# Routing on raw x, with the modulation moved from the tokens into the experts of a hierarchical expert layer

## The chip, the cores and the metric

The kernel runs on one core of a Trainium2 chip. The metric is the device time of one execution in microseconds (us): the median of three runs of the kernel before is 1857.02 us (1854.01 to 1859.16). Engines are called TensorE (PE, matmuls and transposes), VectorE (DVE), ScalarE (ACT), GpSimd (POOL) and SyncE (SP, which issues most DMAs).

## What is computed

The reference is two blocks in a row, over 512 tokens of 1024 numbers in float32. The first block is two layers of attention and is not touched. The second block has two layers, each a mixer followed by a hierarchical mixture of experts; the change is in the latter, which runs once per layer. Cut to that:

```python
def modulate(x, gain, shift, scale):
    return rms_norm_2(x, gain) * (1 + scale) + shift

def hier_moe(h, rg_w, rg_b, re_w, re_b, w_gate, w_up, w_down):
    ...
    g_prob = jax.nn.softmax(t32 @ rg_w + rg_b, axis=-1)
    g_p, g_idx = lax.top_k(g_prob, 1)
    e_logits = (t32 @ re_w + re_b).reshape(n_tok, N_GROUPS, EXPERTS_PER_GROUP)
    e_sel = jnp.take_along_axis(e_logits, g_idx[:, :, None], axis=1)[:, 0]
    top_p, top_i = lax.top_k(jax.nn.softmax(e_sel, axis=-1), TOP_K)
    ...
    def step(acc, xs):
        wg, wu, wd, cw = xs
        y = (jax.nn.silu(t @ wg) * (t @ wu)) @ wd
        return acc + y * cw[:, None], None

h_lat = h_lat + g2 * hier_moe(modulate(h_lat, norm2_g[i], sh2, sc2), *moe_args)
```

There are 16 experts in 4 groups; a token goes to the best group and to the best two of its four experts. An expert is 1024 to 256 (twice, gate and up) and 256 to 1024. With A = gain * (1 + scale), the modulated token is x * rs * A + shift, where rs is one number per token (the reciprocal of its root mean square) and A and shift have one number per column.

## The kernel before, in words

Tokens lie on 128 partitions in four tiles of 128 tokens, x[:, i, :]. Large products are made as three passes over a high and a low part of each operand: `split_to` (L400) writes the high part with a ScalarE copy and the low part with a subtract on VectorE, or on the engine that is passed as `sub`; `mm3` (L347) issues the three matmuls, the two that need only one low part each behind the one of both high parts. Weights come in chunks of 128x1024 (`weights`, L330), in three buffers each for the high and the low part, so that the split of a chunk waits until TensorE is done with the chunk three before it.

`moe` (L1517) does one layer. Its parts, in the order of the work:

- `moe_tables` (L1507) loads, well ahead, the rows A, shift and g2 as broadcast tiles of 128x1024 (tag "mv", three buffers), and small tables; `rw` holds the router's weights.
- The routing is in a block whose order on TensorE, GpSimd, ScalarE and VectorE is the written one (L1783 to L1843). `k.arrive` pulls out the next piece of the mixer before it, whose last matmuls are added to x at L1037. For each tile i: `square` (L1565) sums squares on ScalarE, `scaled` (L1571) multiplies x by A, `turned` (L1544, L1545) transposes that on TensorE and copies it out on ScalarE, `logits` (L1552) and `folded` (L1558) make 20 router logits on TensorE, `rms` takes the reciprocal root in small VectorE steps (L384 to L397), and `modulate` (L1582 on VectorE, or L1584 on ScalarE with L1585 on GpSimd) finishes the token, which SP stores to a DRAM scratch `tscr` (L1587). `route` (L1591 to L1611) ranks the logits, in VectorE operations of at most 80 elements.
- `before`, `spots`, `hot` and `place` (L1618 to L1648) turn the ranks into the list of tokens of each expert; `fetch` (L1670) gathers 128 rows of `tscr` by that list with an indirect DMA from GpSimd. `place(0, ...)` and `fetch` for expert 0 come first, `place(1, 3, ...)` and the fetch for expert 1 behind it. `split0` splits three of the four weight chunks of expert 0 ahead, with the subtract on GpSimd.
- A branch (L1881) handles an expert with over 128 tokens.
- A second block in written order (L1927 to L1932) does five steps of `weigh` (L1683 to L1722, 20 small operations that make the weights of the experts), `turn` of expert 0's tokens, the rest of `weigh`, and `up(0)`.
- Then the experts. `turn` (L1747) transposes the 128 fetched tokens in two halves of 128x512 into PSUM, and `transposed` (L1735) splits each half from PSUM into xTh (ScalarE) and xTl (VectorE). `up` then runs 24 matmuls over four chunks (L350 to L352 into `pss`), `hidden` (L1762 to L1764) makes silu and product, and `down` (L1852) two transposes, eight matmuls (L1865), the weighting into y (L1867, tag "y", four buffers) and `store` (L1847), an indirect DMA that adds y to the output. Here the engines' orders are a planner's, which interleaves `up(e + 1)` with `down(e)`.

## Time and profile before

| | us |
|---|---|
| median of three runs | 1857.02 (1854.01 to 1859.16) |
| the profiled execution, own time | 1858.75 |
| its span | 1857.0 |
| routing and experts of layer 0, about | 1227 to 1445 |
| routing and experts of layer 1, about | 1628 to 1857 |

The rows further down come from one profiled execution and its times are counted from the span's start. A line of a timeline gives start, duration, engine, line of the code, operation, output<-inputs by the program's names, shapes, how many, and in brackets how long the engine was idle before it and what ended that. Back-to-back operations overlap a little, so durations do not add up exactly to the distance of their starts.

### The profile page before, as it was taken

The numbers are of one execution on the slowest core, as the hardware profiler recorded it, in microseconds if no ns is written. First come the engines' busy times: TensorE is split into PE (matmuls) and PEld (weight loads), VectorE is DVE, ScalarE is ACT, GpSimd is POOL, SyncE is SP. The second block draws the span as 40 slices with busy tenths as digits, with TensorE's granted clock in tenths as the row PEclk, the third lists the DMA queues.
The fourth block names the chain that finished last, engine by engine and source line by source line (L and its number), as shares of the span: only waits on it lengthen the run. The fifth ranks groups of instructions, "written<-read, shape, count | busy, mean of one in ns | idle before, by whom it ended". The sixth has DMA issues, their size and how long they took to land. (4 is left out here: it accounts for less than half of the span.)

```text
span 1857.0 us, 25754 instructions
## 1 busy us (share of the span) xinstructions
PE 1705.9 (92%) x9542; PEld 1334.2 (72%) x9542; DVE 1346.4 (73%) x2532; ACT 770.8 (42%) x1345; POOL 278.2 (15%) x242
## 2 busy tenths in 40 slices
PE   7999999999799999999997889987999799969996
PEld 7877777886697777778866767765666587746663
DVE  4577778876646777576677788879877765589774
ACT  4444333333343443323434445553555322145552
POOL 0000000001200000000003452023221122142221
PEclk9999999999999999999998989997999799979998
DMA  5345565664024445554413213147996463169983
GB/s 176 121 135 149 162 206 162 192 193 135 19 73 125 142 143 151 169 165 148 150 46 110 67 47 126 42 170 265 336 341 194 164 215 95 36 247 304 348 295 75
DMA packets 86948, 298.90 MB, mean 161 GB/s; under 512 B 18854, under 2 KB 20694, under 8 KB 78624
## 3 DMA queue, kind: packets, MB, share of 16 engines
q1 hardware_dynamic: 71584, 271.87, 43.8%
q0 software_dynamic: 10704, 19.79, 4.7%
q10 hardware_dynamic: 4528, 5.51, 1.1%
q8 instruction: 78, 1.28, 0.3%
q14 instruction: 54, 0.44, 0.1%
HBM read 280.23 MB, written 24.96 MB: 164 GB/s over the span
## 5 line engine op out<-in xcount | busy, mean ns | idle before, releaser
L401 ACT ACTIVATE whi<-wraw 128x1024 fp32r<-128x1024 f32 (+2 forms) x166 | 171.7, 1036 | 348.1 <-PE psmm L351 241.6
L350 PE MATMUL psmm<-big,whi 128*128 128x512 f32 x672 | 272.9, 406 | 6.8 <-DVE x L668 5.6
L402 DVE TENSOR_TENSOR wlo<-wraw,whi 128x1024 fp32r<-128x1024 f32 (+3 forms) x165 | 200.9, 1219 | 102.3 <-ACT whi L401 89.6
L352 PE MATMUL psmm<-big,wlo 128*128 128x512 f32 x672 | 266.7, 397 | 0.0
L351 PE MATMUL psmm<-big,whi 128*128 128x512 f32 x672 | 266.6, 397 | 0.0
L980 DVE CUSTOM_DVE_ANT_0 wraw<-wraw,sB 128x1024 f32<-128x1024 f32 x96 | 117.1, 1221 | 83.4 <-DMA wraw<-in_mw_dram 82.9
L350 PE MATMUL psmm<-whi,big 128*128 128x256 f32 (+2 forms) x496 | 165.1, 333 | 1.5 <-ACT big L401 1.0
L351 PE MATMUL psmm<-wlo,big 128*128 128x256 f32 (+2 forms) x496 | 160.7, 324 | 4.9 <-DVE wlo L402 4.9
L352 PE MATMUL psmm<-whi,big 128*128 128x256 f32 (+2 forms) x496 | 159.9, 323 | 2.4 <-DVE big L402 2.3
L350 PEld LDWEIGHTS psmm<-big,whi 128*128 128x128 f32 x672 | 127.3, 189 | 35.8 <-issue 4.7
L352 PEld LDWEIGHTS psmm<-big,wlo 128*128 128x128 f32 x672 | 126.9, 189 | 31.1
L351 PEld LDWEIGHTS psmm<-big,whi 128*128 128x128 f32 x672 | 127.4, 190 | 27.9
L1865 PE MATMUL psmm<-wraw,hs 128*128 128x512 f32 x256 | 122.1, 619 | 5.4 <-ACT hs L1857 3.5
L601 POOL DMA_DIRECT2D qk<-rope x40 | 20.5, 515 | 659.2 <-ACT whi L401 286.9
L351 PEld LDWEIGHTS psmm<-wlo,big 128*128 128x128 f32 x496 | 112.1, 226 | 6.2 <-DVE wlo L402 6.0
L352 PEld LDWEIGHTS psmm<-whi,big 128*128 128x128 f32 x496 | 111.5, 225 | 3.2 <-DVE big L402 3.2
L350 PEld LDWEIGHTS psmm<-whi,big 128*128 128x128 f32 x496 | 111.4, 225 | 2.7 <-ACT big L401 1.7
L350 PE MATMUL pss<-whi,xTh 128*128 128x512 f32 x256 | 104.8, 409 | 2.4 <-ACT xTh L401 2.4
L352 PE MATMUL pss<-whi,xTl 128*128 128x512 f32 x256 | 102.4, 400 | 1.7 <-DVE xTl L402 1.7
L351 PE MATMUL pss<-wlo,xTh 128*128 128x512 f32 x256 | 103.4, 404 | 0.0
L856 PEld LDWEIGHTS pspt<-c_ident,pr 128*128 128x128 f32 x512 | 61.3, 143 | 48.2 <-issue 28.9
L402 DVE TENSOR_TENSOR wlo<-bigm,whi 128x1024 fp32r<-128x1024 f32 x64 | 77.9, 1223 | 17.7 <-ACT whi L401 16.2
(384 smaller groups left out, 3659.7 us busy)
## 6 DMA issues: line engine op xcount, KB each, us to landing
wraw<-in_mw_dram SPq DMA_DIRECT2D x96, 512.0 KB
big<-in_me_dram SPq DMA_DIRECT2D x32, 1024.0 KB
bigm<-in_me_dram SPq DMA_DIRECT2D x32, 1024.0 KB
wraw<-in_me_dram SPq DMA_DIRECT2D x64, 512.0 KB
wraw<-in_wqk_dram SPq DMA_DIRECT2D x48, 512.0 KB
wraw<-in_wv_dram SPq DMA_DIRECT2D x24, 512.0 KB
wraw<-in_ow_dram SPq DMA_DIRECT2D x20, 512.0 KB
wraw<-in_wg_dram SPq DMA_DIRECT2D x16, 512.0 KB
```

What stands on the lines that cost most here:

```text
L350: mm(out, lhs[0], rhs[0], start=first, stop=False)
L351: mm(out, lhs[0], rhs[1], start=False, stop=False)
L352: mm(out, lhs[1], rhs[0], start=False, stop=last)
L401: self.nc.scalar.activation(hi, src, AF.Copy)
L402: (sub or self.nc.vector).tensor_tensor(lo, src, hi.bitcast(F32), ALU.subtract)
L601: nc.gpsimd.dma_start(tiles[b][48:80, :], R[b // 4][32 * (b % 4) : 32 * (b % 4) + 32, :])
L856: nc.tensor.transpose(pt[:, j * P : (j + 1) * P], hd.pr[i][:, j * P : (j + 1) * P], ident)
L980: nc.vector.tensor_tensor_reduce(w, w, sB, 1.0, 0.0, ALU.mult, ALU.add, mf[:, j : j + 1])
L1865: nc.tensor.matmul(acc, hs[:, c * P : (c + 1) * P], w[:, c * 512 : (c + 1) * 512], start=c == 0, stop=c == 1)
```

## The change

The router's weights are multiplied by A once (`r3`), so the routing works on raw x: `scaled` is gone, `turned` transposes x itself, with one copy on VectorE and one on ScalarE. What is stored to `tscr` is x * rs (`send`, a scaled copy on ScalarE). A and shift are loaded as columns (`cols`, 128x2x8, one DMA with 4-byte pieces) and are applied in the experts, to the turned tokens, where a column is a partition: eight ScalarE operations of 128x128 per expert (`modulated_`), with the scale and the bias as pointers, into a new tile of tag "y", from which xTh and xTl are then split. The three subtracts of `split0` move from GpSimd to VectorE, two of them into the second block; `place(1, 3, ...)` and the fetch for expert 1 move there too, and `weigh` runs whole behind `turn` and the last `split0`. The order of the first block is rewritten.

```diff
@@ -1498,16 +1498,18 @@
     nc.vector.tensor_tensor(rb, rb, shift, ALU.add)
 
 
-TABLES = ("mv", "iota", "tri", "info", "rw", "fold")
+TABLES = ("mv", "cols", "iota", "tri", "info", "rw", "fold")
 SMALL = ("lg", "sm", "cmp", "rank", "G", "lgr", "gm", "ge", "gsum", "e2", "w1", "w2", "sec", "We", "Ws",
-         "Ab", "pos", "pos16", "most", "over", "oh", "row", "spread", "lgT", "ix", "ws", "vinf", "vpos", "ivx", "ivw",
+         "Ab", "pos", "pos16", "most", "over", "oh", "row", "spread", "lgT", "ix", "ws", "vinf", "vpos", "ivx", "ivw", "sq2",
          "rs_v2", "rs_y2", "rs_h2", "rs_u2")
 
 
 def moe_tables(k, L, rows):
 
     small = lambda shape, nm, dt=F32: k.t(shape, nm, 1, dt)
-    tables = [brow(k, rows[L], j, ("mv", 3)) for j in (4, 3, 5)]
+    cols = small([P, 2, 8], "cols")
+    k.nc.sync.dma_start(cols, rows[L][3:5, :].rearrange("v (c p) -> p v c", p=P))
+    tables = [cols, brow(k, rows[L], 5, ("mv", 3))]
     for shape, nm, dt in (((P, P), "iota", BF16), ((P, 2 * P + 21), "tri", BF16), ((P, 4, 16, 5), "info", BF16), ((P, 256), "rw", F32), ((P, 20), "fold", F32)):
         tables.append(small(shape, nm, dt))
         k.nc.sync.dma_start(tables[-1], k.I["rw"][L][:, 0:256] if nm == "rw" else k.I[nm])
@@ -1519,10 +1521,12 @@
     ident = k.ident
     v = nc.vector
     small = lambda shape, nm, dt=F32: t(shape, nm, 1, dt)
-    A, sh, g2B, iota, tri, info, rw, fold = tables
+    cols, g2B, iota, tri, info, rw, fold = tables
+    sh, A = ([cols[:, j, c : c + 1] for c in range(8)] for j in range(2))
     rb = k.rb
     tscr = k.dr.tile([S, D], F32, name=f"tscr{L}")
     xbuf = k.xbuf if out is None else out
+
 
 
     xgs = [t([P, D], "xg", 4) for _ in range(4)]
@@ -1535,14 +1539,24 @@
     rss, tTs = {}, {}
     lgr, lgs = small([P, 4, 20], "lgr"), {}
 
-    def turned(i, qs=(0, 1)):
-        src = ys[i]
+    r3 = rw.rearrange("p (c e) -> p c e", e=32)
+    v.tensor_tensor(r3, r3, cols[:, 1, :].unsqueeze(2).to_broadcast([P, 8, 32]), ALU.mult)
+
+    def turned(i, engines):
+
         tT = tTs[i] = xgs[i].rearrange("p (c t) -> p c t", c=8)
-        for q in qs:
+        for q, engine in enumerate(engines):
+            if engine is None:
+                continue
             pt = k.bank("pt")
             for j in range(4):
-                nc.tensor.transpose(pt[:, j * P : (j + 1) * P], src[:, (4 * q + j) * P : (4 * q + j + 1) * P], ident)
-            nc.scalar.activation(tT[:, 4 * q : 4 * q + 4, :], pt.rearrange("p (k t) -> p k t", k=4), AF.Copy)
+                c = 4 * q + j
+                nc.tensor.transpose(pt[:, j * P : (j + 1) * P], x[:, i, c * P : (c + 1) * P], ident)
+            dst, src = tT[:, 4 * q : 4 * q + 4, :], pt.rearrange("p (k t) -> p k t", k=4)
+            if engine is v:
+                v.tensor_copy(dst, src)
+            else:
+                engine.activation(dst, src, AF.Copy)
 
     def logits(i):
 
@@ -1561,14 +1575,14 @@
             nc.scalar.activation(lgr[:, i, :], o, AF.Copy)
             lgs[i] = lgr[:, i, :]
 
-    def square(i):
-        nc.scalar.activation(xgs[i], x[:, i, :], AF.Square, scale=float(D ** -0.5), accum_out=ss[:, i : i + 1])
+    sq2 = small([P, 1], "sq2")
+
+    def square(i, half=None):
+        cs = slice(0, D) if half is None else slice(half * 512, half * 512 + 512)
+        nc.scalar.activation(ys[i][:, cs], x[:, i, cs], AF.Square, scale=float(D ** -0.5), accum_out=sq2 if half else ss[:, i : i + 1])
 
     def keep(i):
         nc.sync.dma_start(xbuf[i * P : (i + 1) * P, :], x[:, i, :])
-
-    def scaled(i, engine, cs=slice(0, D)):
-        engine.tensor_tensor(ys[i][:, cs], x[:, i, cs], A[:, cs], ALU.mult)
 
     def rms(i, n):
         def done(rs):
@@ -1577,14 +1591,14 @@
 
         return k.rsqrt_steps(ss[:, i : i + n], n, done)
 
-    def modulate(i, engine, cs=slice(0, D)):
-        if engine is v:
-            v.scalar_tensor_tensor(ys[i][:, cs], ys[i][:, cs], rss[i], sh[:, cs], op0=ALU.mult, op1=ALU.add)
-        else:
-            nc.scalar.activation(ys[i][:, cs], ys[i][:, cs], AF.Copy, scale=rss[i])
-            engine.tensor_tensor(ys[i][:, cs], ys[i][:, cs], sh[:, cs], ALU.add)
-        if cs.stop == D:
-            nc.sync.dma_start(tscr[i * P : (i + 1) * P, :], ys[i])
+    def rms3():
+        v.scalar_tensor_tensor(ss[:, 3:4], sq2, EPS, ss[:, 3:4], op0=ALU.add, op1=ALU.add)
+        yield
+        yield from k.rsqrt_steps(ss[:, 3:4], 1, lambda rs: rss.update({3: rs}), eps=False)
+
+    def send(i):
+        nc.scalar.activation(ys[i], x[:, i, :], AF.Copy, scale=rss[i])
+        nc.sync.dma_start(tscr[i * P : (i + 1) * P, :], ys[i])
 
     def route(i):
 
@@ -1732,11 +1746,19 @@
             nc.sync.dma_start(raw[:, hs], wsrc(e)[:, hs])
         return [raw[:, c * 1024 : (c + 1) * 1024] for c in range(4)]
 
+    def modulated_(xt, q, pt):
+
+        for j in range(4):
+            c = 4 * q + j
+            nc.scalar.activation(xt[:, c, :], pt[:, j * P : (j + 1) * P], AF.Identity, scale=A[c], bias=sh[c])
+
     def transposed(pts):
         xT = (t([P, 8, P], "xTh", 2, F32R), t([P, 8, P], "xTl", 2, F32R))
+        xt = t([P, D], "y", 4).rearrange("p (c t) -> p c t", c=8)
         for q, pt in enumerate(pts):
             ks = slice(4 * q, 4 * q + 4)
-            k.split_to(xT[0][:, ks, :], xT[1][:, ks, :], pt.rearrange("p (k t) -> p k t", k=4))
+            modulated_(xt, q, pt)
+            k.split_to(xT[0][:, ks, :], xT[1][:, ks, :], xt[:, ks, :])
         return xT
 
     def turn(xg):
@@ -1783,64 +1805,54 @@
     with tc.manual_schedule(engines={ENG.PE, ENG.Pool, ENG.Activation, ENG.DVE}):
         k.arrive()
         square(0)
-        scaled(0, v)
         k.arrive()
         square(1)
-        scaled(1, nc.gpsimd)
-        k.arrive(1)
-        run(rms(0, 2))
-        turned(0)
+        turned(0, (v, nc.scalar))
         k.arrive(1)
         logits(0)
         keep(0)
         keep(1)
-        modulate(0, nc.gpsimd)
+        run(rms(0, 2))
+        k.arrive(1)
         square(2)
-        scaled(2, v)
+        turned(1, (v, nc.scalar))
+        send(0)
         k.arrive(1)
         folded(0)
-        turned(1)
-        scaled(3, v, halves[0])
+        logits(1)
+        square(3, 0)
         r2 = rms(2, 1)
         run(islice(r2, 4))
+        turned(2, (v, nc.scalar))
         k.arrive(1)
-        logits(1)
+        square(3, 1)
+        folded(1)
+        turned(3, (nc.scalar, None))
+        logits(2)
         keep(2)
         keep(3)
-        modulate(1, nc.gpsimd)
-        turned(2)
-        square(3)
-        scaled(3, v, halves[1])
-        run(r2)
-        folded(1)
-        modulate(2, v)
-        turned(3)
-        both(rms(3, 1), route(0), route(1))
-        modulate(3, v)
+        turned(3, (None, v))
+        logits(3)
+        both(rms3(), r2, route(0), route(1))
+        folded(2)
+        folded(3)
+        send(3)
+        send(2)
+        send(1)
         if out is None:
             k.next = brow(k, k.rows[1], 1, ("mv", 3)), brow(k, k.rows[1], 0, ("mv", 3))
-        logits(2)
-        logits(3)
-        folded(2)
-        for i in range(2):
+        both(route(2), route(3))
+        for i in range(4):
             before(i)
-        folded(3)
-        for c in range(2):
-            split0(c, nc.gpsimd)
-        both(route(2), route(3))
-        before(2)
-        before(3)
         spots(0, 4)
         hot(first, pos16[:, :, 0:1], 0, 4)
         place(0, 1, 0, 2, first)
         fetch(idx[0], xgs[0])
         for j in range(4):
             second(j)
-        place(1, 3, 0, 2)
-        fetch(idx[1], xgs[1])
-        split0(2, nc.gpsimd)
         v.tensor_scalar(pos, Ab, -8192.0, 8192.0 - 256.0, op0=ALU.mult, op1=ALU.add)
         v.tensor_tensor(pos, pos, rt[:, 0:64].rearrange("p (i e) -> p i e", e=16), ALU.add)
+        split0(0, v)
 
     def store(y, gi):
 
@@ -1898,7 +1910,7 @@
                     pt = k.bank("pt")
                     for j in range(4):
                         nc.tensor.transpose(pt[:, j * P : (j + 1) * P], xg[:, (4 * q + j) * P : (4 * q + j + 1) * P], ident)
-                    k.copy(xT[:, 4 * q : 4 * q + 4, :], pt.rearrange("p (k t) -> p k t", k=4))
+                    modulated_(xT, q, pt)
                 gu = k.bank("s")
                 for c2 in range(4):
                     raw = t([P, 1024], "wraw", 4)
@@ -1925,10 +1937,12 @@
                 store(y, gi)
 
     with tc.manual_schedule(engines={ENG.PE, ENG.Pool, ENG.Activation, ENG.DVE}):
-        steps = weigh()
-        run(islice(steps, 5))
+        split0(1, v)
+        place(1, 3, 0, 2)
+        fetch(idx[1], xgs[1])
         xT = turn(xgs[0])
-        run(steps)
+        split0(2, v)
+        run(weigh())
         hm = up(0, xT)
     for e in range(15):
         if e == 3 and out is None:
```

## Rows read from the trace of the kernel before

**Rows 1.** Busy time of each engine over the span (page, part 1).

```profile
PE 1705.9 (92%) x9542; PEld 1334.2 (72%) x9542; DVE 1346.4 (73%) x2532; ACT 770.8 (42%) x1345; POOL 278.2 (15%) x242
```

**Rows 2.** Table by stage: stretch, length, then busy (x count) of PE, PEld, DVE, ACT, POOL, clock, DMA.

```profile
1241.00:1268.50 27.50, 10.10 (x112) 7.59 (x107) 25.11 (x77) 8.69 (x17) 13.99 (x8) 0.64 0.55 197
...
1340.00:1380.00 40.00, 39.63 (x164) 27.12 (x162) 31.82 (x40) 22.45 (x31) 10.51 (x7) 1.00 0.99 348
...
1642.00:1665.60 23.60, 8.34 (x86) 6.28 (x86) 20.21 (x70) 6.90 (x13) 10.50 (x6) 0.63 0.43 157
```

**Rows 3.** Timeline of VectorE, routing of layer 0.

```profile
1250.30 2.41 DVE L1608 TENSOR_SCALAR G<-rank 128x4 f32<-128x4 f32 x2
...
1252.69 2.42 DVE L1611 SCALAR_TENSOR_TENSOR Ab<-rank,G 128x16 bf16<-128x16 f32 x2
...
1257.88 0.29 DVE L1608 TENSOR_SCALAR G<-rank 128x4 f32<-128x4 f32 x2
...
1269.69 0.21 DVE L1694 TENSOR_TENSOR We<-We,lg 128x64 f32<-128x64 f32 x1
...
1273.20 1.22 DVE L402 TENSOR_TENSOR wlo<-big,whi 128x1024 fp32r<-128x1024 f32 x1
```

**Rows 4.** Timeline of GpSimd, routing of layer 0.

```profile
1250.33 4.67 POOL L402 TENSOR_TENSOR wlo<-big,whi 128x1024 fp32r<-128x1024 f32 x2 [5.00 <-ACT whi L401]
...
1260.40 1.65 POOL L1670 DMA_INDIRECT xg<-tscr,ix  x1 [5.40 <-DVE ix L1648]
```

**Rows 5.** Timeline of TensorE, expert 0, layer 0 and then layer 1.

```profile
1265.20 1.94 PE L1747 MATMUL pspt<-c_ident,xg 128*128 128x128 f32 x8 [2.61 <-DMA xg<-tscr,ix]
...
1275.35 0.48 PE L351 MATMUL pss<-wlo,xTh 128*128 128x512 f32 x1
...
1663.85 1.94 PE L1747 MATMUL pspt<-c_ident,xg 128*128 128x128 f32 x8 [2.67 <-DMA xg<-tscr,ix]
...
1672.31 0.48 PE L351 MATMUL pss<-wlo,xTh 128*128 128x512 f32 x1
```

**Rows 6.** Timeline of SP, tables of layer 1.

```profile
1464.29 14.16 SPq L998 DMA_DIRECT2D mv<-mrow  x3
```

**Rows 7.** Timeline of all engines, one period of the experts in layer 0.

```profile
1344.65 0.48 PE L350 MATMUL pss<-whi,xTh 128*128 128x512 f32 x1
...
1344.93 0.60 ACT L401 ACTIVATE xTh<-pspt 128x512 fp32r<-128x512 f32 x1 [2.79 <-PE pspt L1747]
...
1346.31 1.06 ACT L401 ACTIVATE whi<-bigm 128x1024 fp32r<-128x1024 f32 x1 [0.78 <-PE pss L352]
...
1347.40 1.23 DVE L402 TENSOR_TENSOR wlo<-bigm,whi 128x1024 fp32r<-128x1024 f32 x1 [1.15 <-ACT whi L401]
...
1349.06 0.39 PE L351 MATMUL pss<-wlo,xTh 128*128 128x512 f32 x1
...
1355.00 0.48 PE L350 MATMUL pss<-whi,xTh 128*128 128x512 f32 x1
```

**Rows 8.** Groups of ScalarE by form, whole span: busy, mean ns of one, idle before.

```profile
L401 ACT ACTIVATE xTh<-pspt 128x512 fp32r<-128x512 f32 x64 | 37.6, 596 | 79.0 <-PE pspt L1747 78.8
...
L401 ACT ACTIVATE cath<-gc 128x512 fp32r<-128x512 f32 x16 | 10.1, 631 | 26.0 <-DVE gc L895 14.2 <-DVE gc L897 11.3 <-PE psmm L351 0.4
...
L731 ACT ACTIVATE v<-pspt,gs 128x512 fp32r<-128x512 f32 x10 | 6.4, 686 | 8.8 <-PE pspt L729 8.8
...
L1338 ACT ACTIVATE pr<-pss,mn 128x512 f32<-128x512 f32 x32 | 22.0, 687 | 31.6 <-DVE mn L1336 28.9 <-DVE rs_yn L397 2.7
...
L1584 ACT ACTIVATE y<-y,rs_y 128x1024 f32<-128x1024 f32 x4 | 4.6, 1145 | 1.6 <-DVE rs_y L397 1.6
...
L1554 ACT ACTIVATE lgT<-psmm 128x128 f32<-128x128 f32 x8 | 2.2, 278 | 6.1 <-PE psmm L1552 6.1
```

**Rows 9.** The store of an expert's output (L1847), issue to landing.

```profile
DMA to landing us min/median/max: 6.3/8.5/11.6
```

## The prediction, made before the result was known

> **What bounds the kernel now.** I read the busy times first, then a table by stage over the two passes of the expert layer, then the timelines of the stages that the diff touches. TensorE is busy 92% of the span [rows 1]. In the table by stage the reader is to see two different regimes. In the expert loops TensorE is busy 39.63 of 40 us and ScalarE only 22.45 [rows 2], so nothing moved off another engine can gain anything there, and ScalarE has some 17 us in 40 to give. Between the last matmul of the mixer and the first of expert 0, TensorE works 10.10 of 27.5 us in layer 0 and 8.34 of 23.6 in layer 1, at a granted clock of 0.64 and 0.63, while VectorE works 25.11 and 20.21 [rows 2]. That gap, twice, is the only place where the change can gain, and VectorE's chain sets its length.
>
> In that chain small operations take long while GpSimd works: the two comparisons over 128x4 at L1608 take 2.41 us as a pair, and the next pair, L1611, 2.42, while GpSimd runs its two subtracts of 4.67 us over just that stretch [rows 3, 4]. The chain ends in the fetch of expert 0's tokens at 1260.40, and the transposes of these tokens start 4.80 us later, at 1265.20 [rows 4, 5].
>
> **The change, part by part.** The profiled execution took 1858.75 us (span 1857.0), 1.73 above the median of 1857.02; the sum is made against 1858.75 and then lowered by that.
>
> *Tables.* Two broadcast rows go, one load of 8 KB with 4-byte pieces comes. In layer 1 the rows' three loads held SP for 14.16 us from 1464.29 [rows 6], but the first use is at about 1628, so this lead covers both the old and the new load: nothing. If the small pieces took ten times as long, they would still be covered.
>
> *Router weights.* One 128x256 product on VectorE, well ahead: nothing on the path.
>
> *Routing.* Five scalings and four modulations go, all additions on GpSimd with them, and the three GpSimd subtracts become VectorE's at about 1.22 each [rows 3]. The two pairs at L1608 and L1611 fall back to about 0.29 each, as in their later occurrences, which saves 4.2 us of the chain in layer 0; layer 1 I take as alike. Against it the last mixer matmuls end some 2 us later, because the transposes and the logits are pulled ahead of them, and the sends of rows 3, 2, 1 are now three scaled copies of 1.145 [rows 8] in series on ScalarE, behind the routing's square root, and the fetch waits for the last of them to land. With that wait the fetch comes near 1255.9, 4.5 us earlier. Indices 1 to 3 are moved behind the overflow branch and no longer delay the first fetch, but lie on VectorE after it. I take the transposes at 4 us earlier in both layers: 1261.2 and 1659.85. The bounds are 0 (the sends land as late as the old fetch) and 7 (all held time and the modulations surface).
>
> *What is given back before the fourth chunk.* The new order on VectorE is: split of chunk 1, places of experts 1 to 3, the two lower halves of the tokens, split of chunk 2, all of the twenty weighing steps, and only then the lower part of the fourth weight chunk, which waits behind them; TensorE waits for that. Before, five weighing steps lay ahead of the tokens and the rest took from 1269.69 to 1273.2 [rows 3]. Counted from the first transpose: 1.0 for the first half, two halves of four modulations and a copy (2.2 each, priced below) 4.4, the last lower half 0.69, a split 1.22, the weighing 3.6 and five more steps of some 0.21, so 4.6, the fourth chunk 1.22: 13.1, and 13.5 with a few hops between engines. So its lower part is ready at 1274.7, where it was used at 1275.35 [rows 5], and in layer 1 at 1673.35, where it was used at 1672.31. Of the 4 us nothing is left: -0.65 and +1.04. TensorE starts earlier and then idles, and expert 1's weights queue behind the same VectorE work, for which I add 0.5 per layer: +1.4 in all, say +1.5. The bounds are -8 (the 4 us of each layer survive, because what stands ahead of the chunk is shorter than I price it) and +5 (the clock stays low for longer).
>
> *The modulation in the experts.* This runs 16 times per layer. Each expert's transposed tokens now pass through eight ScalarE operations of 128x128 from PSUM, with a pointer as scale and one as bias, before the copy that splits them. No such operation is in the trace. Without a pointer this size takes 278 ns [rows 8]. One pointer, as scale, takes a 128x512 operation from 596 to 686; as bias, to 687 [rows 8], so 0.09 each. The bounds are 0.278 and 0.46 (both pointers paid in full); I take 0.46, since each pointer alone is seen to cost its 0.09. Successive ones overlap by about the same 0.09, so four take 4 x 0.37 + 0.09 = 1.57. The copy then reads SBUF, 631 for 596 [rows 8]. Eight add 3.0 us to about 5.8 busy (22.45 of 40 [rows 2]) in a period of 10.35, so ScalarE does not become the bound by its sum.
>
> By its order it may. In the steady period (gate matmuls start at 1344.65 and again at 1355.00 [rows 7]) the second half's copy runs from 1344.93 to 1345.53, then ScalarE idles 0.78 until a buffer is free, and splits the fourth chunk from 1346.31; VectorE's part follows from 1347.40 to 1348.63, and TensorE takes it at 1349.06 [rows 7], a slack of 0.43. With the modulations the copy starts at 1344.93 + 1.57 + 0.03 = 1346.53 and ends at 1347.16, the chunk's split begins there, less an overlap of 0.09: 1347.07, which is 0.76 late. Of it 0.43 is cover and 0.33 a stall of TensorE. Nobody gives it back, as TensorE has 0.37 us in 40 idle [rows 2]. Layer 1 I take as alike. Expert 0 runs in the written order and the last one has no successor beside it, so 14 of each layer run in this pattern: 28 x 0.33 = 9.2. At the price of one pointer (0.37) the delay is 0.4, within the cover: nothing. Where each dependent step has another 0.2, or the operation costs 0.55, it is 0.55 to 0.7 per expert: +15 to +20.
>
> The Trainium skill, page "ScalarE: Activation LUTs", section "What ACT_TABLE_LOAD costs", says that each pointer operand adds about 93 ns and gives 186 ns + 0.833 ns per element: 479 ns here as an estimate. The rows on one pointer agree with it (90 ns); the sum by it would be about 2.1 us higher (28 x 4 x 0.019).
>
> The new intermediate tile shares four buffers with the experts' outputs, so an output now waits for the store two experts back, where it waited for the fourth; that store lands in at most 11.6 us [rows 9] and has nearly two periods, 20.7: nothing.
>
> Sum: 1858.75 + 1.5 + 9.2 = 1869.5; against the median 1867.7, given as 1868.
>
> **The rivals.** About 0.3%, 5.6 us, is what a measurement of this kernel can tell from no change.
> - *The modulation fits.* A price near one pointer, or an order in which the fourth chunk's split goes first, leaves the experts as they are, and the routing stage alone moves, within -4 and +4: about 1857. For it: ScalarE has 4 us free per period. Against it: both pointers are seen to cost, and the slack is 0.43.
> - *The routing gain surfaces.* The experts cost nothing and TensorE starts the fourth chunk 4 us earlier in both layers, since the weighing overlaps more than I let it: 1857 - 8 = 1849, the faster side. It decides if VectorE reaches the fourth chunk within 10 us of the first transpose. For it: the held pairs [rows 3]. Against it: the twenty steps are now in one piece ahead of it.
> - *The experts' chain becomes long.* If the split of the fourth chunk is placed ahead of the second half's copy, or the operations cost 0.55, each period grows by 0.55 to 0.9: 28 x 0.7 = 20 and the 1.5, so about 1879.
>
> **How the numbers follow.** Forecast (experts +5 to +13, routing about zero) 0.45; long chain 0.08; modulation fits 0.25, in which the time is within 0.3% nearly always; routing surfaces 0.22, faster. So faster 0.22, same 0.25, slower 0.53. The range takes the low end at 1850, the routing gain almost in full, and the high end at 1881, the long chain; the forecast's own range is 1862 to 1876.
>
> **What would show it.** Right: in the routing stage VectorE's small operations at 0.3, no GpSimd arithmetic, the transposes of expert 0 about 4 us earlier against the last mixer matmul; the modulations at 0.46 each; the period of the experts at about 10.7, with TensorE waiting for VectorE's lower part at the fourth chunk once per expert. Wrong: a period still at 10.35 (the modulation fits), an operation near 0.37, or a gap between mixer and expert 0 that shrinks by 4 us or more and stays shrunk at expert 1.

## The result and the profile after

The kernel after takes 1932.58 us (median, 1922.64 to 1941.57), the kernel before, run beside it, 1855.97. The ratio is 1.041 with an interval of 1.0345 to 1.0474: slower, and outside the range of the prediction. The profiled execution took 1922.64 us, its span is 1920.9, which is 63.9 above that of before. It is the fastest of the four, and the profile therefore shows less than the median's loss: over its span the granted clock is 0.952, and it is 0.943 in the two slowest (1939.29 and 1941.57).

First the busy times and the two groups that bear on the modulation, from the page of the kernel after, which answer to [rows 1] and [rows 8], and last the group of the kernel before that answers to the third line.

```profile
PE 1726.8 (90%) x9542; PEld 1337.1 (70%) x9542; DVE 1327.1 (69%) x2536; ACT 861.6 (45%) x1601; POOL 252.7 (13%) x230
...
L1753 ACT ACTIVATE y<-pspt,cols 128x128 f32<-128x128 f32 x256 | 96.8, 465 | 97.8 <-PE pspt L1769 94.4
...
L402 DVE TENSOR_TENSOR xTl<-y,xTh 128x512 fp32r<-128x512 f32 x64 | 44.1, 691 | 86.8 <-ACT xTh L401 86.7
```

```profile
L402 DVE TENSOR_TENSOR xTl<-pspt,xTh 128x512 fp32r<-128x512 f32 x64 | 43.8, 686 | 10.6 <-ACT xTh L401 10.6
```

ScalarE's 256 new operations (L1753) take 465 ns each, as priced, and ScalarE is far from being the bound. It waits 94.4 us in front of them for TensorE's transposes (L1769, which was L1747); that wait is not new, since the copies that came next before waited 78.8 us there [rows 8]. New is that VectorE then waits 86.7 us for ScalarE, where it waited 10.6. So it has to be asked what TensorE does meanwhile.

The table by stage of the kernel after, columns as in [rows 2], with two short stretches at the end, one from a period in which the clock holds and one from the next gate:

```profile
1241.00:1266.00 25.00, 10.57 (x61) 7.66 (x60) 11.84 (x37) 11.15 (x23) 4.15 (x4) 0.61 0.69 237
...
1340.00:1380.00 40.00, 35.23 (x127) 22.96 (x126) 24.80 (x30) 25.67 (x48) 8.76 (x7) 0.92 0.84 278
...
1780.00:1820.00 40.00, 35.25 (x132) 23.09 (x131) 25.82 (x31) 26.98 (x50) 9.24 (x6) 0.96 0.74 266
...
1350.00:1361.90 11.90, 10.31 (x39) 6.45 (x38) 7.69 (x10) 8.72 (x16) 3.08 (x2) 1.00 0.89 271
1366.90:1369.90 3.00, 3.00 (x9) 2.32 (x7) 1.81 (x2) 1.25 (x2) 0.00 (x0) 0.50 0.57 144
```

In the experts TensorE now works 35.23 of 40 us where it worked 39.63 [rows 2], and the granted clock of the stretch is 0.92 instead of 1.00. The last line resolves that: the clock is not a little low all the time, it stands at 0.50 (1.2 GHz) for about 3 us of a period and at 1.00 (2.4 GHz) otherwise. The waits of TensorE in 1340 to 1420, of which the kernel before has none:

```profile
PE pspt L1867 <- ACT y L1753: 6.9, 6, 1.2
PE pss L350 <- ACT xTh L401: 2.6, 6, 0.4
```

Where in a period these waits lie is seen in the timeline of TensorE, first expert 0, then one period of the kernel after:

```profile
1254.19 1.95 PE L1769 MATMUL pspt<-c_ident,xg 128*128 128x128 f32 x8
1257.59 0.80 PE L350 MATMUL pss<-whi,xTh 128*128 128x512 f32 x1 [1.45 <-ACT xTh L401]
...
1266.70 0.49 PE L350 MATMUL pss<-whi,xTh 128*128 128x512 f32 x1 [1.53 <-ACT whi L401]
1269.11 0.35 PE L1656 MATMUL psav<-info,oh 128*128 128x3 bf16 x8 [1.92 <-DVE info L1736]
1269.32 0.77 PE L350 MATMUL pss<-whi,xTh 128*128 128x512 f32 x1
1270.17 0.79 PE L351 MATMUL pss<-wlo,xTh 128*128 128x512 f32 x1
...
1352.50 0.50 PE L350 MATMUL pss<-whi,xTh 128*128 128x512 f32 x1 [0.43 <-ACT xTh L401]
...
1358.48 3.60 PE L1877 MATMUL psmm<-wraw,hs 128*128 128x512 f32 x8
1361.91 1.04 PE L1769 MATMUL pspt<-c_ident,xg 128*128 128x128 f32 x8
1364.11 0.44 PE L1867 MATMUL pspt<-c_ident,pr 128*128 128x128 f32 x2 [1.16 <-ACT y L1753]
1364.97 0.50 PE L350 MATMUL pss<-whi,xTh 128*128 128x512 f32 x1 [0.43 <-ACT xTh L401]
...
1367.34 0.63 PE L351 MATMUL pss<-wlo,xTh 128*128 128x512 f32 x1
1367.77 0.63 PE L352 MATMUL pss<-whi,xTl 128*128 128x512 f32 x1
...
1372.48 3.59 PE L1877 MATMUL psmm<-wraw,hs 128*128 128x512 f32 x8
```

and the same engine in the kernel before, between the gate matmuls of two experts (they start at 1344.65 and 1355.00 [rows 7]):

```profile
1350.20 0.38 PE L1855 MATMUL pspt<-c_ident,pr 128*128 128x128 f32 x2
1350.41 0.60 PE L1747 MATMUL pspt<-c_ident,xg 128*128 128x128 f32 x4
1351.11 3.70 PE L1865 MATMUL psmm<-wraw,hs 128*128 128x512 f32 x8
1354.64 0.60 PE L1747 MATMUL pspt<-c_ident,xg 128*128 128x128 f32 x4
```

**The order has changed.** Before: gate matmuls, the two transposes of the hidden product (pr), the first half of the next tokens, the eight matmuls of the down projection, the second half, next gate. The first half's copies lie behind 3.53 us of down projection, the second half's behind the first gate matmuls, which don't need them yet. After: gate, down projection, both halves in one go (x8), a wait of 1.16, pr, a wait of 0.43, next gate. The down projection comes before the transposes and covers nothing; transposes, four modulations and a copy stand bare in front of the gate. From the start of the transposes to the gate it is 1364.97 - 1361.91 = 3.06 us, where the same work stood in (1351.11 - 1350.20) + (1355.00 - 1354.64) = 1.27. Then the gate itself takes 1372.48 - 1364.97 = 7.51 us, where it took 5.55. In the period before it, in which the clock holds, the gate takes 1358.48 - 1352.50 = 5.98. The other 1.53 are the clock: after the two waits it falls to 0.50 and the matmuls follow each other every 0.43 us instead of 0.23. So this period is 14.01 us for 10.35: 1.79 from the order, 0.43 from a gate that is slower even at 1.00, 1.53 from the clock, less 0.09 on the down projection. Where the clock holds, a period is 12.45 to 12.48. From expert 4 to expert 14 each layer has ten periods, five of this kind and five of 13.95 to 14.02.

The 63.9 us by stage. The mark is the start of each gate's first matmul with the low part of the weights (L351), since the one before it can stand alone: in the kernel after that of expert 1 starts at 1269.32, among the last of expert 0. To expert 1 of layer 0, -4.7; experts 1 to 15, +31.4; from there to expert 1 of layer 1, +8.5; experts 1 to 15, +29.6; the rest, -0.9.

### The profile page after: what moved, and what is told of

It is laid out like the page before. It is cut to its first block, busy times and chain, and to the rows that moved or that the text cites. A ratio compares the mean times of both kernels' runs of the same rounds, so it can differ in the third digit from the quotient of the medians.

```text
span 1920.9 us, 25945 instructions
## 1 busy us (share of the span) xinstructions
PE 1726.8 (90%) x9542; PEld 1337.1 (70%) x9542; DVE 1327.1 (69%) x2536; ACT 861.6 (45%) x1601; POOL 252.7 (13%) x230
## 5 line engine op out<-in xcount | busy, mean ns | idle before, releaser
L351 PE MATMUL psmm<-big,whi 128*128 128x512 f32 x672 | 266.6, 397 | 0.0
L351 PE MATMUL psmm<-wlo,big 128*128 128x256 f32 (+2 forms) x496 | 162.0, 327 | 5.5 <-DVE wlo L402 5.5
L351 PEld LDWEIGHTS psmm<-big,whi 128*128 128x128 f32 x672 | 127.2, 189 | 27.9
L1753 ACT ACTIVATE y<-pspt,cols 128x128 f32<-128x128 f32 x256 | 96.8, 465 | 97.8 <-PE pspt L1769 94.4
L350 PE MATMUL pss<-whi,xTh 128*128 128x512 f32 x256 | 114.2, 446 | 16.6 <-ACT xTh L401 11.9
L1877 PE MATMUL psmm<-wraw,hs 128*128 128x512 f32 x256 | 117.7, 602 | 1.0 <-ACT hs L1869 0.9
L351 PEld LDWEIGHTS psmm<-wlo,big 128*128 128x128 f32 x496 | 113.4, 229 | 6.8 <-DVE wlo L402 6.6
L352 PE MATMUL pss<-whi,xTl 128*128 128x512 f32 x256 | 114.4, 447 | 1.1 <-DVE xTl L402 1.1
L351 PE MATMUL pss<-wlo,xTh 128*128 128x512 f32 x256 | 111.2, 435 | 0.8 <-DVE wlo L402 0.7
L402 DVE TENSOR_TENSOR xTl<-y,xTh 128x512 fp32r<-128x512 f32 x64 | 44.1, 691 | 86.8 <-ACT xTh L401 86.7
```

What stands on the lines that cost most here:

```text
L350: mm(out, lhs[0], rhs[0], start=first, stop=False)
L351: mm(out, lhs[0], rhs[1], start=False, stop=False)
L352: mm(out, lhs[1], rhs[0], start=False, stop=last)
L402: (sub or self.nc.vector).tensor_tensor(lo, src, hi.bitcast(F32), ALU.subtract)
L1753: nc.scalar.activation(xt[:, c, :], pt[:, j * P : (j + 1) * P], AF.Identity, scale=A[c], bias=sh[c])
L1877: nc.tensor.matmul(acc, hs[:, c * P : (c + 1) * P], w[:, c * 512 : (c + 1) * 512], start=c == 0, stop=c == 1)
```

## The experiments

Periods are the distance of the gate matmuls of successive experts, in the steady part; in the kernel before they are 10.35 in layer 0 and 10.49 in layer 1. A ratio stands with its interval where there were enough runs; the other times are single runs.

**1. Everything but the modulation in the experts** (against the kernel after).

```diff
-        xt = t([P, D], "y", 4).rearrange("p (c t) -> p c t", c=8)
         for q, pt in enumerate(pts):
             ks = slice(4 * q, 4 * q + 4)
-            modulated_(xt, q, pt)
-            k.split_to(xT[0][:, ks, :], xT[1][:, ks, :], xt[:, ks, :])
+            k.split_to(xT[0][:, ks, :], xT[1][:, ks, :], pt.rearrange("p (k t) -> p k t", k=4))
```

> The changed kernel with the experts of before: the eight modulations are left out (so shift and A are missing from the tokens), the tokens are split straight from PSUM; routing and second block as changed. Theory O (the modulations made the planner put both transposes of the next expert behind the down projection, right ahead of the gate matmuls, and TensorE waits there for the whole chain transpose, modulation, copy): the period of the experts is back at 10.35 us and the time is 1850 to 1858. Rival S (the splits and the weighing moved onto VectorE delay the experts): the period stays above 12 and the time above 1900.

1856.18 us, ratio 1.0005 (0.9986 to 1.0024), period 10.50. The order of before is back and the whole loss is gone, so it is not the routing. The gain of the routing is gone too: gate 0 starts 9.3 us earlier than before in layer 0 (1259.21 for 1268.50), gate 1 3.6 earlier (its first low-part matmul, 1273.61 for 1277.16), gate 4 only 0.9 (1311.75 for 1312.68). The table by stage from gate 0 to gate 4, for this kernel and then for the one before:

```profile
1259.00:1312.00 53.00, 47.78 (x237) 32.82 (x236) 44.00 (x77) 24.81 (x36) 13.40 (x10) 0.87 0.78 278
```

```profile
1268.00:1313.00 45.00, 42.79 (x235) 30.07 (x236) 42.42 (x76) 24.04 (x34) 11.77 (x9) 0.95 0.90 319
```

The same 235 or so matmuls take 5.0 us more at 0.87 than at 0.95, and TensorE idles 5.2 us instead of 2.2 (1.6 for the tokens of expert 1, 1.4 and 0.7 for weight chunks). An earlier start only moved it to where it waits.

**2. The modulation alone** (the kernel before, with the column table and the eight ScalarE operations; its tokens are modulated twice).

```diff
             ks = slice(4 * q, 4 * q + 4)
-            k.split_to(xT[0][:, ks, :], xT[1][:, ks, :], pt.rearrange("p (k t) -> p k t", k=4))
+            for j in range(4):
+                c = 4 * q + j
+                nc.scalar.activation(xt[:, c, :], pt[:, j * P : (j + 1) * P], AF.Identity, scale=Ac[c], bias=shc[c])
+            k.split_to(xT[0][:, ks, :], xT[1][:, ks, :], xt[:, ks, :])
```

> The kernel before, routing untouched, with the eight modulations of each expert added (the tokens are modulated twice). O: period 12.4 to 14.3 as in the changed kernel, time 1915 to 1945. S: the period stays near 10.7, time at most 1870.

1931.67 us, periods 12.46 and 13.7 to 14.3: the whole loss, with the old routing. Its TensorE waits are those of the kernel after, 1.16 and 0.43 per expert.

**3. Transposes emitted around the down projection** (the kernel after).

```diff
-            nxt = up(e + 1)
+            nxt = up(e + 1, T[0] if e else None)
...
+            T = begin(e + 2)
+            half(T, 0)
             down(e, hm)
+            half(T, 1)
```

> The changed kernel, with the same operations, but the source emits the transposes and modulations of expert e+2 one step earlier: the first half ahead of the down projection of e, the second behind it. O: TensorE has other work while the modulations run, period 10.4 to 10.9, time 1852 to 1868. Rival P (the eight operations are dear in any order, ScalarE's chain is the bound): period 12 or more, time above 1900.

1876.79 us, ratio 1.0108 (1.0088 to 1.0128), period 10.89, clock 1.00. With all operations in place, putting work between the transposes and their users takes back most of the loss in the experts. In the time it is a miss by some 9 us, and a wait is left per expert, now for VectorE, since the planner put the split of a weight chunk ahead of the tokens' copy:

```profile
PE pss L352 <- DVE xTl L402: 2.0, 7, 0.3
```

**4. The chain without pointers** (the modulations are plain copies; A and the shift are left out).

```diff
-            nc.scalar.activation(xt[:, c, :], pt[:, j * P : (j + 1) * P], AF.Identity, scale=A[c], bias=sh[c])
+            nc.scalar.activation(xt[:, c, :], pt[:, j * P : (j + 1) * P], AF.Copy)
```

> The changed kernel with the eight modulations as plain copies of the same shape, with no scale and no bias pointer (shift and A are left out of the tokens). O (the whole chain transpose, modulation, copy lies bare behind the planner's order): only the length of the chain shrinks, by 4 x 0.19 per half, so the period falls by about 0.8 but stays above 11.4, time 1885 to 1910. Rival P (the pointers' price is what made the loss): the period is back near 10.4, time below 1865.

1876.26 us, period 11.34: below what the theory had stated, in time and in period, and above its rival. In the timeline six of the eight transposes still follow the down projection, and pr still stands in the gap, but the waits of TensorE are shorter and the clock stays at 1.00. The waits in 1340 to 1380, and that stretch in the table by stage:

```profile
PE pspt L1867 <- ACT y L1753: 1.8, 4, 0.4
PE pss L350 <- ACT xTh L401: 1.0, 4, 0.2
...
1340.00:1380.00 40.00, 37.28 (x147) 23.63 (x145) 29.61 (x37) 25.47 (x61) 8.87 (x7) 1.00 0.96 338
```

So 0.68 us of waits per expert cost 1.0 of period and leave the clock; 1.59 cost 2.1 where the clock holds and 3.7 where it falls.

**5. The order alone** (the kernel before, without modulation, both halves and then pr emitted ahead of the gate, the down projection behind it).

```diff
-            nxt = up(e + 1)
+            xT = turn(fetch(idx[e + 1], xgs[(e + 1) % 4]) if e else xgs[1])
+            hs = turned_(hm)
+            nxt = up(e + 1, xT)
...
-            down(e, hm)
+            down(e, hm, hs)
```

> The kernel before, no modulation in the experts, but with the changed kernel's order on TensorE (down projection, both transposes of the next expert, then its gate matmuls). O: what is bare is then only the transposes and one copy, about 0.8 us of idle per expert: period 11.0 to 11.7, time 1875 to 1900. P: the order costs nothing by itself, period 10.35, 1857.

1866.06 us, period 10.75 and 10.85. The order alone costs 0.4 per expert, less than expected, because without the modulations TensorE waits only 0.25 in the gap; pr slipped behind the first gate matmuls, so it is not exactly the order of after. Neither the order nor the longer chain (0.29, experiments 9 and 11) costs much by itself; together they cost 2.1 and then the clock.

**6. The routing's tail ahead of the branch** (kernel 1, with places, weighing and all three splits moved there).

```diff
-        split0(0, v)
+        place(1, 3, 0, 2)
+        fetch(idx[1], xgs[1])
+        run(weigh())
+        for c in range(3):
+            split0(c, v)
```

> The kernel of e1 (experts without modulation) with the places of experts 1 to 3, the fetch for expert 1, the weighing and all three splits moved ahead of the overflow branch, into the time in which VectorE waits for TensorE's branch. Theory G (the routing's gain was given back because this work stood behind the branch, ahead of the fourth chunk): expert 1's gate matmuls start near 1267 in layer 0 against 1272.3 in e1, time 1843 to 1851. Rival B (what TensorE's branch and the slow clock take comes back whatever the order; the first experts absorb it): 1853 to 1858.

1851.78 us, ratio 0.9968 (0.995 to 0.9987). The transposes of expert 0 come at 1266.92 instead of 1257.43, but gate 4 starts at 1314.30, 2.6 later than in kernel 1 and 1.6 later than before. Expert 1's gate starts at 1278.48, where the theory had 1267. The gain is small and does not lie in layer 0 where it was looked for. It is the only kernel here whose interval lies below 1, by 0.3%, and it leaves the modulation out.

**7 and 8. The halves inside the gate** (after its second and fourth chunk, order left to the planner; 8 has the tail of kernel 6 as well).

```diff
+            for q in range(2):
+                if T and (1, 3)[q] == c1:
+                    half(T, q)
```

> The changed kernel, the same operations, with both halves of expert e+2 emitted inside the gate matmuls of e+1 (behind its second and its fourth chunk). O: the whole chain of both halves is covered by matmuls, period 10.4 to 10.6, time 1855 to 1866. P: ScalarE is 9.4 of 10.35 busy and delays the weight splits whatever the order: period 10.8 or more, time 1870 or more.

> The kernel of e7 with the work ahead of the branch as in e6; all of the reference is computed. G and O together: 1845 to 1857, as fast as before or a little faster. B with O: 1855 to 1866, as e7.

1884.18 us, 1.0148 (1.0117 to 1.0179), and 1881.2, 1.0125 (1.0092 to 1.0157); period 11.39 in both. The times are those of 7's rival P, but its reason, that ScalarE delays the splits in any order, does not hold (10 below). The hope that more distance hides more failed, since the planner again chose the order: it put the down projection behind the first matmuls of the next gate, and these wait 0.62 per expert for VectorE's lower part of the tokens.

**9 and 11. The order of before, written by hand on all four engines** for experts 1 to 15, with the modulation (9) and without (11).

```diff
+            gate(gu, X, 3, xT, W[X, 3])
+            nxt = hidden(gu)
+            hs = down_open(e, hm)
+            if more:
+                pt = half_t(N, 0)
...
+            acc = down_mm(hs, ws[1])
+            if more:
+                pt = half_t(N, 1)
```

> The changed kernel, all of its operations, with experts 1 to 15 in an order written by hand on all four engines: that of the kernel before (gate matmuls, transposes of the hidden tile, first half of the next tokens, down projection, second half). This is the order on which the prediction's 0.33 per expert was worked out. Theory O (the prediction's price was right and its order was not): period 10.6 to 10.8, time 1858 to 1868. Rival Q (the price in that order was mis-sized too): period above 11.0, time above 1873.

> The kernel of e9 without the modulations (the tokens are split straight from PSUM; shift and A are missing). The control for e9: O and Q both expect the period of before, 10.35 to 10.5, and 1853 to 1862; if it is longer, e9's excess is the hand order's and not the modulation's.

Times 1914.64, 1.0301 (1.0277 to 1.0324), and 1879.09. The totals say little, because the steps that place the tokens of experts 2 to 15 were threaded in crudely: in 9 the four periods from gate 1 on are 15.0 to 20.2. From gate 7 on they are what this was for: 10.79 with the modulation, 10.50 without. In the order of before the modulation costs 0.29 per expert. It does so at the place that the prediction named, the low part of the fourth weight chunk, whose first matmul starts 0.42 us behind the one before it in 9, and 0.23 in 11:

```profile
1399.32 0.40 PE L350 MATMUL pss<-whi,xTh 128*128 128x512 f32 x1
1399.74 0.50 PE L351 MATMUL pss<-wlo,xTh 128*128 128x512 f32 x1
```

```profile
1390.77 0.39 PE L350 MATMUL pss<-whi,xTh 128*128 128x512 f32 x1
1391.00 0.40 PE L351 MATMUL pss<-wlo,xTh 128*128 128x512 f32 x1
```

**10, 12 to 16. An order made for the modulation.** The first half is transposed after the first gate chunk of the expert before, the second after the third, with pr beside it; 10 has the tail of kernel 6.

```diff
+            gate(gu, X, 0, xT, W[X, 0])
+            if more:
+                pt = half_t(N, 0)
...
+            gate(gu, X, 2, xT, W[X, 2])
+            hs = down_open(e, hm)
+            if more:
+                pt = half_t(N, 1)
```

> The changed kernel with the work ahead of the branch as in e6 and experts 1 to 15 in another order by hand: the transposes of expert e+1 lie behind the first and third chunk of e, so that its modulations run while TensorE has matmuls, and the fourth chunk's split goes ahead of the modulations. O: the modulation can be hidden altogether, period 10.35 to 10.5, time 1846 to 1857. Rival Q (ScalarE, some 9.4 of 10.35 busy, cannot keep up in any order): period 10.9 or more, time 1868 or more.

1875.61 us, 1.0113 (1.008 to 1.0147). The first periods are again spoilt (16.1, then 13.5 three times), the steady one is 10.12. The table by stage:

```profile
1340.00:1380.00 40.00, 40.00 (x165) 27.50 (x164) 32.62 (x45) 34.13 (x64) 9.02 (x6) 1.00 0.98 338
```

ScalarE works 34.13 of 40 and TensorE 40.00, with no wait: the modulation is hidden but for at most 0.07 us (against 14 below) and the period is shorter than before's 10.35. The buffers that the new tile shares with the outputs hold nothing up, as the prediction had it. The time is a miss all the same. The remaining runs tried to get to that order sooner: 12 leaves experts 1 to 5 to the planner, 13 threads the places in earlier, 15 the fetches too; 14 and 16 are the kernel before, routing and all, in the orders of 13 and 15.

```diff
+            if X > 1:
+                fetches(X)
...
+                tick()
+                tick()
```

> The changed kernel with the work ahead of the branch (as e6), experts 1 to 5 as in e7 (the planner's order, halves inside the gate matmuls, so that the places of the later experts can be fitted in) and experts 6 to 15 in the hand order of e10, whose period was 10.12. O: ten periods of 10.12 per layer in place of 10.35 to 10.5, and a start no worse than before: 1840 to 1852, faster than both kernels. Rival B (the planner's first experts or the seam between the two schedules give it back): 1855 to 1866.

> The changed kernel as in e10 (hand order for experts 1 to 15, work ahead of the branch), with the places of the later experts issued one step further ahead of the matmuls that read them, and the fetches earlier. In e10 the first four experts took 16.1 and three times 13.5 where before took 11.1, 12.2, 12.6 and 11.3. O: they come to 11 to 12.5 each, the others stay at 10.12, time 1850 to 1863. Rival B (VectorE, with the places, is the bound there): 13 and more as in e10, time 1870 or more.

> The kernel before, untouched in its routing and without modulations in the experts, all of the reference computed, with the hand order of e13 for its experts. It tells whether the period of 10.12 has anything to do with the change. O (the order alone makes it): period 10.1, time lower than e13 or within 0.5% of it, 1845 to 1860. Rival (the eight modulations cost something even in this order): period below 10.0.

> The changed kernel as in e13, with the places of experts 4 to 7 finished in the middle of expert 2 and their fetches issued there. In e13 TensorE waited 5.4 us for the tokens of expert 4 (period 18.8, in layer 1 14.9). O: these come to 11 to 14, the rest as e13, time 1850 to 1860, no slower than before. Rival B (VectorE is what the first experts wait for, the fetch only stands in for it): 1862 or more.

> The kernel before (its routing, no modulation in the experts) with the same order as e15. O: 4 to 8 us below e14 (1858), so 1848 to 1855, and within 0.3% of e15: the change is worth nothing either way once the order is the same. If it is lower than e15 by more than 0.5%, the modulation keeps a price.

| | us | ratio | steady period |
|---|---|---|---|
| 12 | 1864.46 | 1.004 (1.0025 to 1.0055) | 10.12 |
| 13 | 1864.48 | 1.0051 (1.0031 to 1.007) | 10.12 |
| 14 | 1858.32 | 1.0019 (1.0002 to 1.0035) | 10.05 and 10.12 |
| 15 | 1864.01 | 1.0048 (1.0031 to 1.0065) | 10.12 |
| 16 | 1861.08 | 1.003 (1.0015 to 1.0045) | 10.05 and 10.12 |

All have the short period and none the time, because the first experts take longer: the four periods from gate 1 of layer 0 on are together 53.9 us in 13 and 51.1 in 15, where they are 47.1 in the kernel before. In 15 TensorE waits there mostly for VectorE's steps of the places (3.7 us), in 13 for expert 4's tokens, ahead of its first transposes:

```profile
1306.31 1.09 PE L1777 MATMUL pspt<-c_ident,xg 128*128 128x128 f32 x4 [5.45 <-DMA xg<-tscr,ix]
```

What these runs tell is the price of the change itself. In one and the same order of the experts the ratios of 15, with it, and 16, without it, are 0.0018 apart, those of 13 and 14 0.0032: some 3 to 6 us of the loss are left once the order is taken from the planner. The intervals overlap in both pairs, so this rest is hardly told from nothing. A complete version that beats the kernel before was not found.

## Why the prediction was wrong

- **Tables and router weights: right.** The column load holds SP for 0.40 us (L1511, mean of two) and lands in 3.1 to 4.8 us, long before its use.
- **The price of the modulation: right.** 465 ns for 0.46 taken; its copy 653 ns for 631. The Trainium skill, page "ScalarE: Activation LUTs", section "What ACT_TABLE_LOAD costs", made it 479 ns, as an estimate from its two pointer costs; the trace is 3% below that.
- **The routing: near in the net, by luck.** The term was +1.5; measured to expert 1 it is -4.7 in layer 0 and +8.5 in layer 1, together +3.8, so two errors cancel. Experiment 1 shows the whole routing part at 1.0005. The held pair fell to 0.23 and 0.25 us in layer 0 (0.29 was forecast), and GpSimd has no arithmetic left there. In layer 0 the transposes of expert 0 came 11.0 us earlier: 4.1 against the mixer's last matmul, as forecast, and 6.9 because that matmul itself came earlier (1233.63 for 1240.53; 2 later was forecast). Layer 1 was taken as alike and was not. The fetch is issued 13.8 us behind the mixer's last matmul there, where it was 19.9, but takes 9.8 us to land, where it took 4.7, so that the transposes come only 1.0 earlier against that matmul; why it lands so late was not looked into. The rows after and, behind them, before (1663.85 stands in [rows 5]):

```profile
1666.41 0.40 PE L352 MATMUL psmm<-whi,catl 128*128 128x512 f32 x1
1680.25 1.44 POOL L1684 DMA_INDIRECT xg<-tscr,ix  x1 [55.51 <-DVE oh L1645]
1690.16 1.94 PE L1769 MATMUL pspt<-c_ident,xg 128*128 128x128 f32 x8 [7.90 <-DMA xg<-tscr,ix]
```

```profile
1639.11 0.40 PE L352 MATMUL psmm<-whi,catl 128*128 128x512 f32 x1
1658.98 1.62 POOL L1670 DMA_INDIRECT xg<-tscr,ix  x1 [5.58 <-DVE ix L1648]
```

That an earlier start is given back was forecast by the right means, the weighing ahead of the last chunk ([1.92 <-DVE info] in the timeline above), but mis-sized: from the first transpose to the chunk's low part 13.5 us were worked out, and 16.0 (1254.19 to 1270.17) and in layer 1 16.6 were measured. The clock and the wait for expert 1's tokens add to it.
- **The step that failed** is the one that begins "By its order it may", with its 28 x 0.33 = 9.2. It took the positions of the transposes, copies and splits in the period of before [rows 7] and moved only their ends. The order in the experts is a planner's, and with the longer chain it came out as another one: the down projection ahead of the transposes, and TensorE waiting 1.16 and 0.43 us per expert. The term measured 31.4 + 29.6 = 61.0. Within its assumption the step holds: in the order of before the modulation costs 10.79 - 10.50 = 0.29 us (9 against 11), at the chunk that it named, where 0.33 was worked out.
- **The clock was not in the sum.** Of a long period's loss, 1.53 of 3.66 us is the fall of the clock after the new waits; over the ten long periods counted above that is some 15 of the 61.0 us, as an estimate. The prediction counted a wait as its own length.
- **The rival "the experts' chain becomes long"** named the right place and a change of order, but on ScalarE, one split against one copy, with +20. What moved was TensorE's order, and it was worth three times that. "The modulation fits" would have been right in the order of 10, in which ScalarE's spare time was enough, as the table by stage had suggested.

Why the planner chose so is argued, not shown. The longer chain opens a gap on TensorE between the transposes and the gate; pr, which is ready, fills it; thereby the next down projection is ready straight after the gate, goes ahead of the transposes, and the gap is there again in every expert. That the order is decided by the length of the chain fits experiments 1, 2 and 4 (none, full and half); the planner's own reckoning is not in a trace.

## What to carry to other kernels

Where a planner sets the order, a longer operation is an input to the order as well as a duration: price the addition in the old order, then ask what else could be ready in the gap that it opens, and give an order change a chance and a price of its own. In the trace of after, compare the sequence of the bounding engine over one period before any duration; here four lines of it told more than all groups. Cover is work that stands between a producer and its user, so spare time on an engine hides a chain only if the chain starts early enough. Waits on TensorE can be paid a second time in the clock that follows them, here with 1.53 us in half of the steady periods.

## What the runs showed of the hardware that was not expected

**The clock after short waits.** After two waits of 1.16 and 0.43 us, TensorE having run at 1.00 before, the granted clock stood at 0.50 (1.2 GHz) for some 3 us of a gate. It did so in ten of the twenty steady periods of the kernel after (13.95 to 14.02 us) and not in the ten others (12.45 to 12.48), with the same waits, and no run shows what decides between the two; after waits of 0.44 and 0.24 (experiment 4) the stretch shows 1.00 throughout.

**TensorE's branch on the overflow.** The line's instructions in the kernel after and in the one before (min, median and max in ns):

```profile
L1893 PEldq COMPARE_BRANCH  x2: 349/3383/6417, 1245.5 to 1678.0; - x2
```

```profile
L1881 PEldq COMPARE_BRANCH  x2: 540/765/990, 1262.9 to 1661.3; - x2
```

In layer 0 of the kernel after it takes 6.4 us, in layer 1 0.35, and VectorE, whose own branch is done in 0.07, waits 5.66 us behind TensorE's:

```profile
1252.11 2.50 DVE L1645 TENSOR_TENSOR oh<-iota,pos 128x512 bf16<-128x512 bf16 x4 [5.66 <-PEq L1893]
```

Experiment 1 has it at 3.7 and 6.3 us. The Trainium skill, page "Runtime: NRT & Kernel Launch", section "Instruction fetch mechanics", says that a taken branch out of the prefetched window waits for its target to be fetched by DMA. The spread would fit a fetch that queues behind the weights' loads, but no run here separates that, and it stays open. The places of experts 1 to 3 stand behind it and ahead of expert 0's transposes, which start at 1254.19; the fetch, issued at 1247.38, took 4.9 us to land, so at most 2 us of the routing's gain went there.

**The short period.** That the experts run at 10.12 us with the modulation, below the 10.35 of a kernel without it, was not expected. It is the order's doing, since the kernel before has 10.05 and 10.12 in it (14). Part of it can be read from the rows: in the kernel before the down projection starts at 1351.11, as soon as ScalarE's copy of its input is there, and in 10 that copy is done 1.25 us before the down projection starts (kernel before, then kernel 10):

```profile
1350.68 0.38 ACT L1857 ACTIVATE hs<-pspt 128x256 f32<-128x256 f32 x1
```

```profile
1380.39 0.39 ACT L1806 ACTIVATE hs<-pspt 128x256 f32<-128x256 f32 x1 [0.33 <-PE pspt L1804]
...
1382.03 3.60 PE L1818 MATMUL psmm<-wraw,hs 128*128 128x512 f32 x8
```
